# State of the delta rule by pairs of heads on the whole array, and new numbers for the planner of a hybrid decoder layer

## The chip, the core and the metric

The kernel runs on one core of one Trainium2 chip. The metric is device time in microseconds (us) of one execution. TensorE (PE) does the matmuls, ScalarE (ACT) and VectorE (DVE) do the work on elements, GpSimd (POOL) a few pieces, and SyncE (SP) issues most DMAs. "PEld" in views is PE's loading of weights.

## The reference

One decoder layer for 256 tokens and 1024 channels in float32. The input is multiplied by one large matrix; the columns feed four groups of six heads of 64 channels each: block attention (a), a state space model (s), dilated attention (c) and the gated delta rule (d). Their outputs stand side by side, are multiplied by `w_out`, added to the scaled input and normalised.

```python
proj = x @ w_in                       # (256, 1024) @ (1024, about 5,900)
y_a = moba_attention(...) * silu(a_g)
y_b = rms_norm(ssd_mixer(...) * silu(s_z), ssm_norm_w)
y_c = dilated_attention(...) * silu(c_g)
o_d = gated_delta_chunked(dq, dk, dv, d_beta, d_logdecay)
y_d = rms_norm(o_d, dn_norm_w) * silu(d_g)
mix = concatenate([y_a, y_b, y_c, y_d]) @ w_out
return layer_norm(DEEPNORM_ALPHA * x + mix, ln_g, ln_b)
```

The delta rule goes over chunks and carries a 64x64 state `St` for each head; the change is in the product that makes the state for the second chunk:

```python
v_new = uc - wc @ St
o = (qc * exp(gc)) @ St + ac @ v_new
St = St * exp(glast) + einsum("bhcd,bhce->bhde", kc * exp(glast - gc), v_new)
```

## The kernel before

**Staging.** The big products run as three: each weight block is loaded as float32 into a `raw` buffer, ACT rounds it to `whi` (fp32r), DVE subtracts to give `wlo`, and PE multiplies x high by `whi`, x low by `whi` and x high by `wlo`. There are four buffers each of `raw`, `whi` and `wlo`, so a load waits for the split of the block four before it, and a split waits until PE has read the block four before it. SP issues all these loads, and those of biases, in one fixed order. PSUM has eight banks (`ps0` to `ps7`); a tile of any kind takes a bank until its last reader is done.

**Order.** The kernel's functions do not run instructions, they record them in a `Plan`. `Plan.run` then sorts them, engine by engine, with a model of costs, and all are issued from line 381. At each step it takes an instruction by rank, which is the length of the model's work behind it plus a bias: `PRIO` gives one per stage ("attention a", "delta"), `STEPS` one per step of a stage and engine. `LIMIT` says how many banks a kind of tile may hold at once ("m" are the products of the delta rule, "g" gates, "a" scores of attention a). `AHEAD` lets an engine take a more important instruction that is ready a little later than another. `STICK` favours, on PE, an instruction that uses the same part of the array as the one before, when that is not the whole array:

```python
def stay(o):
    return int(STICK * 1000) if o["mode"] and o["mode"] == mode != (128, 128) else 0
rank = [-int(o["way"] * 1000 + 0.5) - math.floor(o["bias"] * 1000 + 0.5) for o in ops]
```

**Stages in the order of time.** "conv" and "gate" stages project the delta rule's q, k, v and its decays (to about 60 us). "products" (62 to 72 us) are twelve float32 matmuls `kq x kT` of 64 rows, each of which fills a bank that DVE turns into a block of `M` and one of `A`. Then come projections for s, c and a. "blocks" is a long chain on DVE over `Ub`, which inverts the triangular blocks (to 138 us). "attention c" (about 119 us on) and "attention a" (about 144 us on): PE makes scores, DVE adds a bias and takes the row maximum (a custom instruction that reads `biasc` or `biasa`), ACT takes the exponential and scales (`p`), PE transposes `p`. "join" (154 us on) ends the inverse: `TZ x M`, a copy of `TZ`, `U x TZ`, a copy of `U`. "delta" goes through two chunks of two halves: `vb x U` gives `u`, ACT copies it, `u x M` corrects the next half, DVE subtracts it from `vb`. After the first chunk `u x kdec` makes the state, DVE copies it to `St`, and `St x kbg` and `St x EQ` use it in the second. "out" multiplies by `w_out` (170 to 224 us), "ln" normalises and stores.

Of the kernel before, what the change touches and what calls it, by code (L numbers as in the profile page):

```python
# [16 lines left out]
S, DM, NH, HD = 256, 1024, 6, 64  # L17
W = NH * HD
# [32 lines left out]
def _biases():  # L51
# [12 lines left out]
NSM = 478  # L64
WARM = 8
STREAM = 1.0
SWITCH, PORT, AHEAD = 0.17, 0.9, {"dve": 0.033, "pe": 0.172, "pool": 0.066}
CUTS = (((0, 512), (512, 512)), ((0, 512), (512, 256), (768, 256)))
SHARE = [[slice(a, b) for a, b in v] for v in (
    ((0, 256), (256, 512)), ((512, 1024),), ((0, 512), (512, 1024)), ((0, 384), (384, 768), (768, 1024)))]  # L70
HELD = 5
HOLD = {10: (("hold_hi", "cvg", 1), ("hold_lo", "s3", 1))}
PRIO = {"split": -6.8, "conv k": 146.3, "gate d": -1265.8, "conv q": 1492.8, "gate s": 701.0, "steps": 1693.7,
        "decay d": 1542.9, "norm k": 4481.3, "products": 382.5, "norm q": 5697.9, "decay s": -3554.0,
        "values c": 663.3, "conv v": 174.6, "blocks": 42.6, "join": -2709.8, "delta": 4073.4, "conv bc": 149.8,
        "conv x": -58.8, "state": -630.8, "scan": 3483.0, "scores c": -913.9, "attention c": 9085.5,
        "scores a": 5133.5, "values a": -8452.1, "attention a": 1239.3, "out": -958.7, "out 0": -3694.0,
        "out 1": -5902.3, "ln 0": -1382.8, "ln 1": -1514.8}
CONST = -5, -4, -3
NRAW = 4  # L80
POOL = (6,)
POOLS = {"ps": (8, 512, F), "work": (3, W, F), "workd": (2, W, F), "workx": (1, W, F), "workg": (2, W, F), "cy": (3, S, F), "p": (3, W, F), "mx": (3, 4, F), "pt": (3, W, F), "oss": (2, 6, F), "sss": (2, 1, F), "srs": (2, 1, F)}
RINGS = {"raw": 4, "whi": 4, "wlo": 4}
STEPS = {"conv q 0": {"pe": -2.7}, "gate s 4": {"dve": -198.5}, "products 2": {"dve": 421.0},
# [9 lines left out]
         "attention a 5": {"dve": 0.6, "act": 142.2}, "attention a 6": {"act": -596.3},  # L94
         "attention a 10": {"act": -288.8}, "out 4": {"pe": 22.2}}
LIMIT = {"pj": 6, "g": 3, "ed": 6, "es": 6, "n": 4, "m": 5, "d": 2, "o": 4, "td": 2, "b": 1, "s": 2, "ts": 5, "c": 3, "ct": 6, "cv": 4, "a": 6, "at": 1, "av": 1}
BEGIN, SLOW = 1.2, 2.5
BESIDE = {(64, 128): 0.85, (128, 64): 0.62}
STICK = 1.0


class Plan:
# [70 lines left out]
    def add(self, eng, call, cost, outs, ins, dma=0.0, mode=None, port=False, place=None, slow=0.0):  # L173
        i = len(self.ops)
        if self.found:
            self.ops.append({"id": i, "call": call, "dma": dma})
            return
        deps = {} if self.after is None else {self.after: 0.0}
        op = {"id": i, "bias": self.bias + STEPS.get(self.step, {}).get(eng, 0.0), "stream": self.stream, "eng": eng, "call": call, "cost": cost, "dma": dma,
              "mode": mode, "port": port, "place": place, "slow": slow, "deps": deps, "succ": [], "homes": []}  # L180
# [40 lines left out]
    def run(self):  # L221
# [22 lines left out]
        vacant = {t: list(range(v[0])) for t, v in POOLS.items()}  # L244
        kinds = dict(LIMIT)
        turn = {}
# [21 lines left out]
        def stay(o):  # L268

            return int(STICK * 1000) if o["mode"] and o["mode"] == mode != (128, 128) else 0  # L270

# [120 lines left out]
def hybrid_layer(ctx, tc, plan, xT, x, w_in, w_out, convw, small, ln_g, ln_b, cst, biases, out):  # L392
    nc = tc.nc
    pe, act, dve, pool, sp = (plan.engine(n, e) for n, e in (
        ("pe", nc.tensor), ("act", nc.scalar), ("dve", nc.vector), ("pool", nc.gpsimd), ("sp", nc.sync)))
    pj = plan.engine("pe", nc.tensor, True)
# [5 lines left out]
    def part(name):  # L402
        plan.bias = PRIO.get(name, 0.0)
        plan.stage = plan.step = name

    def step(n):
        plan.step = "%s %d" % (plan.stage, n)

    def new(name, *shape, dt=F, tag=None, bufs=1):
        return plan.tile(sb, (128,) + shape, dt, name, tag, bufs)  # L410

    def bank(kind):
        return plan.tile(ps, (128, 512), F, "ps_" + kind, "ps", kind=kind)

    def work(n=W, tag="work"):
        return new(tag, W)[:, :n]

    def f32(ap):
        return ap.bitcast(F)
# [27 lines left out]
    def split(src, parts=None, tags=None):  # L447
# [3 lines left out]
                  for t, g, b in (tags or (("whi", None, 1), ("wlo", None, 1))))  # L451
        plan.bias += PRIO["split"]
        for r, c in parts or ((slice(0, k), slice(0, n)),):
            act.activation(hi[:, r, c], src[:, r, c], AF.Copy)
            (pool if count in POOL else dve).tensor_sub(lo[:, r, c], src[:, r, c], f32(hi[:, r, c]))
        plan.bias -= PRIO["split"]
        count += 1
# [33 lines left out]
    b = bank("pj")  # L491
# [244 lines left out]
    b = bank("ed")  # L736
# [6 lines left out]
    kbg, kdec = new("kbg", 3, 128), new("kdec", W)  # L743
    for i in range(2):
        b = bank("n")
# [12 lines left out]
        b = bank("n")  # L758
# [6 lines left out]
    for i in range(2):  # L765
        for pr in range(3):
            step(3 * i + pr)
            gb = [bank("m"), bank("m")]
            for g, q in zip(gb, halves):
                pe.matmul(g[:, 0:256], kT[q, pr, i * 128:(i + 1) * 128], kq[q, pr, i].rearrange("p a b -> p (a b)"),  # L770
                          start=True, stop=True)
            for e in range(2):
                h = 2 * pr + e
# [4 lines left out]
    for i in range(2):  # L778
        b, sq = bank("n"), work()
# [17 lines left out]
    for i in range(2):  # L797
        b = bank("n")
# [21 lines left out]
    for j in range(31, 0, -1):  # L820
        n = 32 - j
# [13 lines left out]
    b = bank("d")  # L835
# [5 lines left out]
    b = bank("d")  # L841
# [7 lines left out]
    u = new("u", 2, W, tag="s2")  # L849
    St = new("St", 3, 2, HD)  # L850
    pool.memset(St, 0.0)
    mix[9] = new("mix9", 2, 3, S, dt=R)
    for i in range(2):
        if i:
            b = bank("d")
            for k in range(3):
                pe.matmul(b[:, k * 128:(k + 1) * 128], kbg[:, k, :], St[:, k].rearrange("p e d -> p (e d)"),
                          start=True, stop=True)
            dve.tensor_sub(vb[:, 1, :], vb[:, 1, :], b[:, :W])
        for r in range(2):  # L860
            step(4 * i + r)
            tp = slice(64 * r, 64 * r + 64)
            if r:
                b = bank("d")
                for h in range(NH):
                    hs = slice(h * HD, h * HD + HD)
                    pe.matmul(b[tp, hs], M[0:64, 6 * i + h, tp], u[0:64, i, hs], start=True, stop=True)
                dve.tensor_sub(vb[tp, i, :], vb[tp, i, :], b[tp, :W])
            b = bank("d")
            for h in range(NH):  # L870
                hs = slice(h * HD, h * HD + HD)
                pe.matmul(b[tp, hs], U[tp, 6 * i + h, tp], vb[tp, i, hs], start=True, stop=True)
            act.activation(u[tp, i, :], b[tp, :W], AF.Copy)
        if i == 0:
            b = bank("d")
            for h in range(NH):
                q = slice(64 * (h % 2), 64 * (h % 2) + 64)
                hs = slice(h * HD, h * HD + HD)
                pe.matmul(b[q, (h // 2) * HD:(h // 2) * HD + HD], kdec[:, hs], u[:, 0, hs], start=True, stop=True)
            for e in range(2):  # L880
                q = slice(64 * e, 64 * e + 64)
                dve.tensor_copy(St[q, :, e, :], b[q, :3 * HD].rearrange("p (k d) -> p k d", k=3))
        step(4 * i + 2)
        ob = bank("o")
        for k in range(3):
            if i:
                pe.matmul(ob[:, k * 128:(k + 1) * 128], qg[:, k, :], St[:, k].rearrange("p e d -> p (e d)"),
                          start=True, stop=False, skip_group_check=True)
            for h in (2 * k, 2 * k + 1):
                hs = slice(h * HD, h * HD + HD)  # L890
                pe.matmul(ob[:, hs], A[:, 6 * i + h, :], u[:, i, hs], start=(i == 0),
                          stop=(i == 0 or h % 2 == 1), skip_group_check=True)
        sq, y = work(tag="workd"), work(tag="workd")
        ss = new("oss", 6)
        act.activation(sq, ob[:, :W], AF.Square)
        dve.tensor_reduce(ss, h6(sq), op=OP.add, axis=AX.X)
        dve.scalar_tensor_tensor(ss, ss, 1.0 / 4096, qn[:, i, :], op0=OP.mult, op1=OP.add)
        rsqrt(ss, ss)
        dve.tensor_scalar(ss, ss, 0.0625, None, op0=OP.mult)
        dve.tensor_mul(h6(y), h6(ob[:, :W]), hb(ss))  # L900
        dve.tensor_mul(y, y, gd[:, i, :])
        to_mix("d", y, i, 9)
# [13 lines left out]
    b = bank("b")  # L916
# [3 lines left out]
    b = bank("b")  # L920
# [4 lines left out]
    for i in range(2):  # L925
        for g in range(2):
            s = slice(6 * i + 3 * g, 6 * i + 3 * g + 3)
# [3 lines left out]
    for i in range(2):  # L931
        b = bank("b")
# [6 lines left out]
    b = bank("b")  # L939
    for g in range(2):  # L940
        pe.matmul(b[:, g * 192:(g + 1) * 192], btok[:, g * 128:(g + 1) * 128], Xd[:, g * 192:(g + 1) * 192],
                  start=True, stop=True)
# [3 lines left out]
    for i in range(2):  # L946
        y = yd[:, i, :]
        step(i)
        b = bank("s")
        for h in range(NH):  # L950
            hs = slice(h * HD, h * HD + HD)
            pe.matmul(b[:, hs], Es[:, 6 * i + h, :], X[:, i, hs], start=True, stop=True)
        dve.tensor_add(y, b[:, :W], y)
        if i == 1:
            b = bank("s")
            for g in range(2):
                pe.matmul(b[:, g * 192:(g + 1) * 192], bcT[:, 2 + g, 128:256], st[:, g * 192:(g + 1) * 192],
                          start=True, stop=True)
# [12 lines left out]
    bc = new("biasc", NH, 256, tag="s3")  # L971
# [131 lines left out]
```

## Time and profile before

| | |
|---|---|
| time, median of 3 runs | 232.57 us (232.31 to 232.76) |
| the profiled execution's own time | 233.04 us |
| its span, first to last instruction | 231.3 us |
| mean granted TensorE clock | 0.994 |
| busy: PE, DVE, ACT, POOL | 218.9, 174.5, 140.0, 24.2 us |
| last matmul starts at | 223.93 us |

The span is what the trace covers; 1.7 us of the execution's own time lie around it. Windows are in us from the span's start.

### The profile page before, as it was taken

The numbers are of one execution on the slowest core, as the hardware profiler recorded it, in microseconds if no ns is written. First come the engines' busy times: TensorE is split into PE (matmuls) and PEld (weight loads), VectorE is DVE, ScalarE is ACT, GpSimd is POOL, SyncE is SP. The second block draws the span as 40 slices with busy tenths as digits, with TensorE's granted clock in tenths as the row PEclk, the third lists the DMA queues.
The fourth block names the chain that finished last, engine by engine and source line by source line (L and its number), as shares of the span: only waits on it lengthen the run. The fifth ranks groups of instructions, "written<-read, shape, count | busy, mean of one in ns | idle before, by whom it ended". The sixth has DMA issues, their size and how long they took to land. (4 is left out here: it accounts for less than half of the span.)

```text
span 231.3 us, 4530 instructions
## 1 busy us (share of the span) xinstructions
PE 218.9 (95%) x1679; PEld 202.6 (88%) x1679; DVE 174.5 (75%) x414; ACT 140.0 (61%) x297; POOL 24.2 (10%) x28
## 2 busy tenths in 40 slices
PE   8999999999999999999989999798999999999970
PEld 3999899998989999999979998687889998888870
DVE  2764999998599989998999984351677996635274
ACT  4765965738953666754469936999932854442210
POOL 7005021200110000000000000000221300000071
PEclk9999999999999999999999999999999999999997
DMA  5999766893934975489550249940523052663013
GB/s 170 312 335 361 209 195 201 211 241 81 273 102 102 234 187 155 128 225 277 150 163 29 68 101 320 270 110 9 180 67 119 1 184 91 211 242 94 0 68 113
DMA packets 46101, 38.10 MB, mean 165 GB/s; under 512 B 5616, under 2 KB 42608, under 8 KB 46080
## 3 DMA queue, kind: packets, MB, share of 16 engines
q1 hardware_dynamic: 45648, 37.43, 55.2%
q10 hardware_dynamic: 432, 0.39, 0.5%
q8 instruction: 13, 0.21, 0.4%
q14 instruction: 8, 0.07, 0.1%
HBM read 36.18 MB, written 1.64 MB: 163 GB/s over the span
## 5 line engine op out<-in xcount | busy, mean ns | idle before, releaser
L381 ACT ACTIVATE whi<-raw 128x1024 fp32r<-128x1024 f32 (+3 forms) x57 | 56.9, 1004 | 40.9 <-PE ps L381 31.1
L381 DVE TENSOR_TENSOR wlo<-raw,whi 128x1024 fp32r<-128x1024 f32 (+3 forms) x56 | 64.2, 1154 | 21.3 <-ACT whi L381 17.5
L381 PE MATMUL ps<-xhi,whi 128*128 128x256 f32 x272 | 41.9, 289 | 0.2
L381 PE MATMUL ps<-xlo,whi 128*128 128x256 f32 x272 | 41.8, 286 | 0.0
L381 PE MATMUL ps<-xhi,wlo 128*128 128x256 f32 x272 | 39.8, 284 | 0.0
L381 PEld LDWEIGHTS ps<-xhi,whi 128*128 128x128 f32 x272 | 36.0, 190 | 2.6 <-ACT whi L381 1.5
L381 PEld LDWEIGHTS ps<-xlo,whi 128*128 128x128 f32 x272 | 36.4, 191 | 0.8 <-issue 0.3
L381 PEld LDWEIGHTS ps<-xhi,wlo 128*128 128x128 f32 x272 | 35.7, 189 | 0.0
L381 PE MATMUL ps<-whi,mix 128*128 128x512 f32 (+1 forms) x110 | 28.7, 350 | 0.0
L381 ACT ACTIVATE p<-p,mx 128x256 f32<-128x256 f32 (+1 forms) x48 | 19.5, 444 | 3.6 <-DVE mx L381 3.6
L381 PEld LDWEIGHTS ps<-whi,mix 128*128 128x128 f32 x110 | 19.1, 188 | 2.7
L381 DVE SCALAR_TENSOR_TENSOR cy<-ps,cw,cy 128x253 f32<-128x253 f32 (+2 forms) x48 | 20.8, 473 | 0.8 <-ACT cy L381 0.7
L381 PE MATMUL ps<-wlo,mix 128*128 128x512 f32 (+1 forms) x55 | 19.3, 350 | 0.0
L381 PE MATMUL ps<-whi,xlo 128*128 128x384 f32 (+2 forms) x64 | 17.3, 344 | 0.0
L381 PE MATMUL ps<-whi,xhi 128*128 128x384 f32 (+2 forms) x64 | 16.9, 345 | 0.0
L381 PE MATMUL ps<-wlo,xhi 128*128 128x384 f32 (+2 forms) x64 | 16.4, 340 | 0.0
L381 POOL TENSOR_SCALAR_AFFINE_SELECT Es<-Es 128x1536 f32<-128x1536 f32 x1 | 1.5, 1548 | 100.7 <-ACT Es L381 100.7
L381 PEld LDWEIGHTS ps<-whi,xlo 128*128 128x128 f32 x64 | 11.6, 188 | 0.1
L381 PEld LDWEIGHTS ps<-wlo,xhi 128*128 128x128 f32 x64 | 11.6, 188 | 0.1
L381 PEld LDWEIGHTS ps<-whi,xhi 128*128 128x128 f32 x64 | 11.2, 188 | 0.5 <-ACT whi L381 0.2
L381 PEld LDWEIGHTS ps<-wlo,mix 128*128 128x128 f32 x55 | 10.4, 188 | 1.4
L381 DVE TENSOR_TENSOR Ub<-Ub 48x31 f32<-48x31 f32 (+15 forms) x31 | 10.3, 332 | 0.7
(219 smaller groups left out, 309.4 us busy)
## 6 DMA issues: line engine op xcount, KB each, us to landing
raw<-in_w_in_dram SPq DMA_DIRECT2D x30, 512.0 KB, 4.4
raw<-in_w_out_dram SPq DMA_DIRECT2D x12, 512.0 KB, 3.4
raw<-in_w_in_dram SPq DMA_DIRECT2D x8, 384.0 KB, 3.3
lead<-in_w_in_dram SPq DMA_DIRECT2D x7, 256.0 KB, 5.0
raw<-in_w_in_dram SPq DMA_DIRECT2D x4, 396.0 KB, 6.6
raw<-in_w_in_dram SPq DMA_DIRECT2D x4, 390.0 KB, 4.7
x<-in_x_dram SPq DMA_DIRECT2D x2, 512.0 KB, 5.1
xr<-in_xT_dram SPq DMA_DIRECT2D x7, 128.0 KB, 5.0
```

Source lines behind the costliest of these rows:

```text
L381: self.plan.add(eng, lambda: f(*a, **k), cost, outs, ins, dma, mode, port or (eng == "pool" and not dma), place, slow)
```

## The change

The state's product takes two heads at a time: three matmuls of the whole 128x128 array in place of six of a 64 column part. The blocks off the diagonal, products of one head's keys with the other's values, are made and not read: the two copies to `St` take the diagonal. A step mark is gone. All tables of the planner have new values; a few lines of them stand here.

```diff
-SWITCH, PORT, AHEAD = 0.17, 0.9, {"dve": 0.033, "pe": 0.172, "pool": 0.066}
+SWITCH, PORT, AHEAD = 0.17, 0.9, {"pe": 0.175}
...
-LIMIT = {"pj": 6, "g": 3, "ed": 6, "es": 6, "n": 4, "m": 5, "d": 2, "o": 4, "td": 2, "b": 1, "s": 2, "ts": 5, "c": 3, "ct": 6, "cv": 4, "a": 6, "at": 1, "av": 1}
+LIMIT = {"pj": 5, "g": 6, "ed": 5, "es": 5, "n": 3, "m": 4, "d": 4, "o": 5, "td": 2, "b": 1, "s": 1, "ts": 4, "c": 6, "ct": 3, "cv": 4, "a": 5, "at": 1, "av": 1}
...
-STICK = 1.0
+STICK = 1000.0
...
         if i == 0:
             b = bank("d")
-            for h in range(NH):
-                q = slice(64 * (h % 2), 64 * (h % 2) + 64)
-                hs = slice(h * HD, h * HD + HD)
-                pe.matmul(b[q, (h // 2) * HD:(h // 2) * HD + HD], kdec[:, hs], u[:, 0, hs], start=True, stop=True)
+
+            for k in range(3):
+                c = slice(k * 128, k * 128 + 128)
+                pe.matmul(b[:, c], kdec[:, c], u[:, 0, c], start=True, stop=True)
             for e in range(2):
                 q = slice(64 * e, 64 * e + 64)
-                dve.tensor_copy(St[q, :, e, :], b[q, :3 * HD].rearrange("p (k d) -> p k d", k=3))
-        step(4 * i + 2)
+                dve.tensor_copy(St[q, :, e, :], b[q, :W].rearrange("p (k a d) -> p k a d", k=3, a=2)[:, :, e, :])
```

The order moves in most stages between 27 us and 201 us; the first 159 and the last 123 instructions of PE stand as before. Three places are shown. Numbers behind names are those of buffers.

On PE the products stood in three groups, five, six and one, between projections. Before:

```order
L381 MATMUL ps3_97<-kq_94,kT_93 128x256
L381 MATMUL ps7_120<-kq_94,kT_93 128x256
L381 MATMUL ps2_99<-kq_94,kT_93 128x256
L381 MATMUL ps5_105<-kq_94,kT_93 128x256
L381 MATMUL ps6_106<-kq_94,kT_93 128x256
L381 MATMUL ps1_96<-xhi_87,whi_187 128x256
L381 MATMUL ps0_86<-xhi_87,whi_190 128x256 x8
L381 MATMUL ps0_86<-xlo_88,whi_190 128x256 x8
L381 MATMUL ps0_86<-xhi_87,wlo_191 128x256 x8
L381 MATMUL ps6_106<-kq_94,kT_93 128x256
L381 MATMUL ps4_98<-kq_94,kT_93 128x256
```

After, the same place:

```order
L381 MATMUL ps6_106<-kq_94,kT_93 128x256
L381 MATMUL ps2_99<-kq_94,kT_93 128x256
L381 MATMUL ps3_97<-kq_94,kT_93 128x256
L381 MATMUL ps5_105<-kq_94,kT_93 128x256
L381 MATMUL ps0_86<-xhi_87,whi_187 128x256 x8
L381 MATMUL ps0_86<-xlo_88,whi_187 128x256 x8
L381 MATMUL ps0_86<-xhi_87,wlo_188 128x256 x2
L381 MATMUL ps1_96<-kq_94,kT_93 128x256
L381 MATMUL ps7_120<-kq_94,kT_93 128x256
L381 MATMUL ps4_98<-kq_94,kT_93 128x256
L381 MATMUL ps6_106<-kq_94,kT_93 128x256
```

Four products now stand ahead of 18 matmuls of a projection, and eight in a row follow (four more behind those shown).

On DVE, ahead of attention a, the splits `wlo_298` and `wlo_301` stood apart in the chain over `Ub`. SP issues the load `raw_308` when the first is done, `raw_311` when the second is, and then `biasa`, the biases that attention a adds. Before:

```order
L381 TENSOR_TENSOR wlo_298<-raw_296,whi_297 128x768
L381 TENSOR_TENSOR work1_155<-ps6_106,cg_164 128x256
L381 TENSOR_TENSOR Ub_202<-BL_201,Ub_202 48x156
L381 TENSOR_TENSOR Ub_202<-Ub_202 48x6x26
L381 TENSOR_TENSOR Ub_202<-BL_201,Ub_202 48x135
L381 TENSOR_TENSOR work2_156<-ps4_98,cg_164 128x256
L381 TENSOR_TENSOR Ub_202<-Ub_202 48x5x27
L381 TENSOR_TENSOR Ub_202<-BL_201,Ub_202 48x112
L381 TENSOR_TENSOR Ub_202<-Ub_202 48x4x28
L381 TENSOR_TENSOR Ub_202<-BL_201,Ub_202 48x87
L381 TENSOR_TENSOR wlo_301<-raw_299,whi_300 128x768
```

After, the same place:

```order
L381 TENSOR_TENSOR Ub_202<-BL_201,Ub_202 48x156
L381 TENSOR_TENSOR work1_155<-ps2_99,cg_164 128x256
L381 TENSOR_TENSOR Ub_202<-Ub_202 48x6x26
L381 TENSOR_TENSOR Ub_202<-BL_201,Ub_202 48x135
L381 TENSOR_TENSOR Ub_202<-Ub_202 48x5x27
L381 TENSOR_TENSOR Ub_202<-BL_201,Ub_202 48x112
L381 TENSOR_TENSOR work2_156<-ps7_120,cg_164 128x256
L381 TENSOR_TENSOR Ub_202<-Ub_202 48x4x28
L381 TENSOR_TENSOR wlo_301<-raw_299,whi_300 128x768
L381 TENSOR_TENSOR Ub_202<-BL_201,Ub_202 48x87
L381 TENSOR_TENSOR wlo_298<-raw_296,whi_297 128x768
```

Both splits now stand late in the chain, `wlo_301` first, and SP issues `raw_311`, `raw_308` and `biasa` in that order.

On PE, join and delta, from the copy of `U` to the state's use. Before:

```order
L381 MATMUL ps3_97<-xhi_87,whi_309 128x256
L381 MATMUL ps5_105<-vb_195,U_196 64x64 x6
L381 MATMUL ps3_97<-xhi_87,whi_309 128x256 x5
L381 MATMUL ps6_106<-u_204,M_157 64x64 x6
L381 MATMUL ps3_97<-xhi_87,whi_309 128x256 x2
L381 MATMUL ps3_97<-xlo_88,whi_309 128x256 x4
L381 MATMUL ps5_105<-vb_195,U_196 64x64 x6
L381 MATMUL ps4_98<-xhi_87,whi_312 128x256 x6
L381 MATMUL ps6_106<-u_204,kdec_153 64x64 x6
L381 MATMUL ps5_105<-u_204,A_158 128x64 x4
L381 MATMUL ps2_99<-St_205,kbg_152 128x128 x3
```

After, the same place:

```order
L381 MATMUL ps7_120<-xhi_87,whi_309 128x256 x6
L381 MATMUL ps3_97<-vb_195,U_196 64x64 x6
L381 MATMUL ps7_120<-xhi_87,whi_309 128x256 x2
L381 MATMUL ps7_120<-xlo_88,whi_309 128x256 x3
L381 MATMUL ps4_98<-u_204,M_157 64x64 x6
L381 MATMUL ps7_120<-xlo_88,whi_309 128x256 x5
L381 MATMUL ps7_120<-xhi_87,wlo_310 128x256
L381 MATMUL ps3_97<-vb_195,U_196 64x64 x6
L381 MATMUL ps7_120<-xhi_87,wlo_310 128x256 x7
L381 MATMUL ps6_106<-xhi_87,whi_312 128x256 x5
L381 MATMUL ps4_98<-u_204,kdec_153 128x128 x3
L381 MATMUL ps3_97<-u_204,A_158 128x64 x5
```

The matmuls `St x kbg` follow the five of `A`. Ahead of `vb x U`, `u x M` and the state there are now 6, 5 and 18 matmuls of projections in place of 1, 5 and 12. On ACT the split `whi_322`, of a block of `w_out` that is wanted later, now stands ahead of the second copy of `u`; on DVE its `wlo_323` stands ahead of the copies to `St`.

## Rows read from the trace of the kernel before

**Rows 1.** The page, busy time and share of the span of each engine.
```profile
PE 218.9 (95%) x1679; PEld 202.6 (88%) x1679; DVE 174.5 (75%) x414; ACT 140.0 (61%) x297; POOL 24.2 (10%) x28
```
**Rows 2.** What PE waited for: total us, times, longest.
```profile
PE ps L381 <- ACT p L381: 2.7, 3, 1.2
```
**Rows 3.** Timeline of PE at conv q: start, busy us, instruction, [idle before].
```profile
26.85 0.51 PE L381 MATMUL ps<-xlo,whi 128*128 128x256 f32 x3
27.47 1.22 PE L381 MATMUL ps<-xhi,whi 128*128 128x256 f32 x8
```
**Rows 4.** Timeline of DVE and PE around the decays' transposes.
```profile
53.63 1.23 DVE L381 TENSOR_TENSOR wlo<-raw,whi 128x1024 fp32r<-128x1024 f32 x1 [0.70 <-ACT whi L381]
...
54.85 0.16 DVE L381 COPY cumd<-ps 128x12 f32<-128x12 f32 x1
...
55.16 0.38 PE L381 MATMUL ps<-csb,cumd 128*6 128x128 f32 x2 [0.47 <-DVE cumd L381]
```
**Rows 5.** Timeline of PE at the products; each product shows as two rows.
```profile
61.81 1.11 PE L381 MATMUL ps<-xhi,wlo 128*128 128x256 f32 x8
62.85 1.56 PE L381 MATMUL ps<-kq,kT 64*128 64x256 f32 x10
...
67.49 1.73 PE L381 MATMUL ps<-kq,kT 64*128 64x256 f32 x12
69.15 1.09 PE L381 MATMUL ps<-xhi,whi 128*128 128x256 f32 x7
70.18 0.70 PE L381 MATMUL ps<-kq,kT 64*128 64x256 f32 x2
70.80 1.22 PE L381 MATMUL ps<-xlo,whi 128*128 128x256 f32 x8
```
**Rows 6.** Timeline of DVE at the products.
```profile
64.10 1.46 DVE L381 TENSOR_TENSOR wlo<-raw,whi 128x1024 fp32r<-128x1024 f32 x1 [0.52 <-ACT whi L381]
...
66.32 1.11 DVE L381 SCALAR_TENSOR_TENSOR M<-ps,rk,Ed 128x128 f32<-128x128 f32 x4
```
**Rows 7.** Timelines of DVE, SP, ACT and PE ahead of attention a.
```profile
132.75 0.96 DVE L381 TENSOR_TENSOR wlo<-raw,whi 128x768 fp32r<-128x768 f32 x1
...
138.24 0.34 SPq L381 DMA_DIRECT2D biasa<-in_biases_dram  x1
...
144.05 0.42 DVE L381 CUSTOM_DVE_ANT_0 p<-ps,biasa 128x256 f32<-128x256 f32 x1 [0.83 <-DMA biasa<-in_biases_dram]
...
144.52 0.51 ACT L381 ACTIVATE p<-p,mx 128x256 f32<-128x256 f32 x1 [2.02 <-DVE mx L381]
...
147.13 0.55 PE L381 MATMUL ps<-csb,p 128*128 128x128 f32 x3 [1.24 <-ACT p L381]
```
**Rows 8.** DMA issues from 130 to 150 us: count, KB each, us from issue to landing.
```profile
raw<-in_w_in_dram SPq DMA_DIRECT2D x3, 512.0 KB, 4.3
biasa<-in_biases_dram SPq DMA_DIRECT2D x1, 768.0 KB, 5.7
```
**Rows 9.** Timeline of PE in join and delta.
```profile
160.16 0.91 PE L381 MATMUL ps<-vb,U 64*64 64x64 f32 x12 [0.54 <-ACT U L381]
...
162.12 0.91 PE L381 MATMUL ps<-u,M 64*64 64x64 f32 x12 [0.27 <-ACT u L381]
...
165.71 0.57 PE L381 MATMUL ps<-u,kdec 128*64 128x64 f32 x12
166.21 1.10 PE L381 MATMUL ps<-u,A 128*128 128x64 f32 x8
167.37 0.94 PE L381 MATMUL ps<-St,kbg 128*128 128x128 f32 x6
168.14 0.56 PE L381 MATMUL ps<-u,A 128*128 128x64 f32 x4
```
**Rows 10.** Timelines of ACT and DVE in delta.
```profile
165.68 1.06 ACT L381 ACTIVATE whi<-raw 128x1024 fp32r<-128x1024 f32 x1
...
166.32 0.72 DVE L381 COPY St<-ps 64x192 f32<-64x192 f32 x2 [1.29 <-PE ps L381]
```

More of the change, by code (lines that the diff above doesn't have):

```diff
@@ L72 @@
 HOLD = {10: (("hold_hi", "cvg", 1), ("hold_lo", "s3", 1))}
[L73 to L78, printed above, removed]
+PRIO = {"split": -6.8, "conv k": -839.0, "gate d": -1623.0, "conv q": 3038.6, "gate s": 708.5, "steps": 2655.8,
+        "decay d": 1955.6, "norm k": 4396.4, "products": 252.7, "norm q": 5719.5, "decay s": -3877.9,
+        "values c": 581.4, "conv v": 156.6, "blocks": -701.0, "join": -3665.0, "delta": 5543.6, "conv bc": 87.4,
+        "conv x": -23.6, "state": -57.6, "scan": 4309.6, "scores c": -1661.9, "attention c": 8479.5,
+        "scores a": 4875.0, "values a": -8056.3, "attention a": 113.3, "out": -847.7, "out 0": -3284.5,
+        "out 1": -7153.9, "ln 0": -1284.1, "ln 1": -492.7}
 CONST = -5, -4, -3
@@ L83 @@
 RINGS = {"raw": 4, "whi": 4, "wlo": 4}
-STEPS = {"conv q 0": {"pe": -2.7}, "gate s 4": {"dve": -198.5}, "products 2": {"dve": 421.0},
[9 rows of a table removed]
-         "attention a 5": {"dve": 0.6, "act": 142.2}, "attention a 6": {"act": -596.3},
-         "attention a 10": {"act": -288.8}, "out 4": {"pe": 22.2}}
-LIMIT = {"pj": 6, "g": 3, "ed": 6, "es": 6, "n": 4, "m": 5, "d": 2, "o": 4, "td": 2, "b": 1, "s": 2, "ts": 5, "c": 3, "ct": 6, "cv": 4, "a": 6, "at": 1, "av": 1}
+STEPS = {"gate s 3": {"dve": 111.0}, "gate s 4": {"dve": -194.3}, "products 2": {"dve": 332.3},
[11 rows of a table added]
+LIMIT = {"pj": 5, "g": 6, "ed": 5, "es": 5, "n": 3, "m": 4, "d": 4, "o": 5, "td": 2, "b": 1, "s": 1, "ts": 4, "c": 6, "ct": 3, "cv": 4, "a": 5, "at": 1, "av": 1}
 BEGIN, SLOW = 1.2, 2.5
 BESIDE = {(64, 128): 0.85, (128, 64): 0.62}
-STICK = 1.0
+STICK = 1000.0
 class Plan:
```

20 rows, old and new, of the table STEPS are left out of this document.

## The prediction

> **What bounds the kernel now.** I read the page first. TensorE is busy for 95% of the span [rows 1], so time is won only where PE stands still, where it changes the part of the array that it uses, or where it has less to do. The view of waits comes next: its largest item is 2.7 us in three stops for ACT's exponentials [rows 2]. The timeline of PE then places the stops: 1.24 us at attention a's first transpose [rows 7], 0.54 and 0.27 in join and delta [rows 9], 0.47 at the decays' transposes [rows 4], and a start at 27.47 that is late against the pace [rows 3]. That pace: eight matmuls of 256 columns take from 61.81 to 62.85 [rows 5], less about 0.1 for the switch at the end, so 0.118 us each; by columns one of 384 takes 0.177.
>
> The stops have late partners, and these decide what a new order is worth. At attention a DVE waits for the transfer of `biasa` and starts at 144.05; ACT starts at 144.52 [rows 7], and its timeline shows no idle row from there to the second copy of `u`, which ends at about 165.7, where the next split starts [rows 10]. The state's product starts on PE at 165.71 [rows 9]. So from 144 to 166 us ACT's queue is the chain, and PE's stops are where it catches up with that queue. A stop that is filled with other matmuls comes back at the next copy, unless ACT's work ahead of that copy is shorter too.
>
> **The state's product.** Twelve rows take from 165.71 to 166.21, 0.50 us [rows 9]. After the change there are three matmuls of 128 columns on the whole array, six rows; the nearest row is `St x kbg`, the same shape, six rows from 167.37 to 168.14, 0.77 us (with a restart of about 0.1 taken off it is 0.67). Bounds: 0.67 to 0.77, so a loss of 0.17 to 0.27. The change of array part in front of it goes; what that is worth is bounded by zero and by a whole excursion, 0.41 (below). I take half, 0.2, and get a loss of about 0.05. The copies to `St` keep their size, two in 0.72 [rows 10]; what is read is strided otherwise, for which no row has a price: I take nothing, with 0.1 as an upper bound.
>
> The Trainium skill (TensorEngine Tiling (Array Packing), Performance Considerations) offers 2x for a tiled output of 64 columns, which speaks against this change: by that rule the whole-array form would take 1.0 us, and the sum below would be 0.25 lower, a forecast of 232.8. By the rows it is 0.77 at most: the tiled form gains a factor of 1.3 to 1.5 here and not 2, and the sum stays as it is below.
>
> **Conv q.** After three matmuls from 26.85 the next was due at 27.20 and starts at 27.47 [rows 3], 0.27 late, for a split on ACT. After the change the first block's 24 matmuls run on. That gains 0 to 0.37 (with a restart of 0.1). The splits on ACT keep their order and PE arrives at the next one sooner, so I take 0.15.
>
> **Decays.** PE waits 0.47 for `cumd`, which stands on DVE behind a split of 1.23 us begun at 53.63 [rows 4]. In the order after, this split is still ahead, and five matmuls of 384 in place of six lie between. That costs 0.18; one split of the stage is also moved later on DVE, and with it the load behind it. Range -0.6 to 0, taken -0.25.
>
> **Products.** Two rows take 0.62 (70.18 to 70.80), twelve take 1.66 (67.49 to 69.15) [rows 5]: 0.104 a row and 0.41 for going there and back. Two excursions in place of three save 0.41. Against this, each product needs two DVE operations, four of which take 1.11 [rows 6], so about 0.53 a product where PE needs 0.21. DVE begins after the split that starts at 64.10 and takes 1.46, at 65.5. The last of the eight needs bank `ps1` again, which the first of the eight used: eight operations of the first four products and three more come before it is free, at 65.5 + 11 x 0.265 = 68.4. PE comes there at 62.85 + 0.2 + 8 x 0.104 + 0.2 + 18 x 0.118 + 0.2 + 14 x 0.104 = 67.9. So it waits about 0.5 (0 to 0.8). Net -0.1.
>
> **Attention a.** PE has ten matmuls of 384 in place of five between the last work of the scores and the first transposed `p`. That covers 0.88 of the 1.24 and is worth nothing by itself, since the chain is ACT's. What counts is when `biasa` lands. It is issued at 138.24 [rows 7] and takes 5.7 us [rows 8]. Before, the load `raw_308` could go out at about 133.7, after a split begun at 132.75 and lasting 0.96 [rows 7], and with 4.3 us [rows 8] it landed at about 138.0, before `biasa` was issued. Now it goes out only after `wlo_298`, late in the chain over `Ub`, right before `biasa`: 512 KB more in front of it. But `raw_311`, of the same size, goes out earlier. If the two merely trade places the cost is 0; if not, 256 KB more cost 5.7 - 4.3 = 1.4 us by rows 8, so 512 KB up to 2.8. The exchange is the nearer case; I take -0.15.
>
> **Join and delta.** Until the second copy of `u` ACT does what it did before and one split more, 1.06 [rows 10]: the state can start 1.0 later. By then PE has done 29 matmuls of 256 columns where it had done 18 (11 x 0.118 = 1.30), so the work stands 0.3 further on. The stops for `U` and `u`, 0.54 and 0.27, are covered or paid on the way there and aren't counted again. Behind the state, `St x kbg` began 0.22 late (eight rows of `A` from 166.21 at 0.117 end at 167.15; start 167.37) [rows 9]; five matmuls of `A` in place of four, 0.23, cover that: +0.2. On DVE `wlo_323` now stands before the copies to `St`; its split is the one ahead of `u` on ACT, and it ends near 167.4, when the product is done too. Taken together +0.5, from -0.4 (the split late by a DVE slot) to +1.1.
>
> **Out.** PE shows no stop there; four splits stand in another order, and POOL's order is unchanged. Taken -0.05 (-0.3 to 0.2).
>
> **The sum.** -0.05 + 0.15 - 0.25 - 0.1 - 0.15 + 0.5 - 0.05 = 0.05 us gained: nothing that counts. The profiled execution takes 233.04, 0.47 more than the median of the runs, 232.57; the same difference applies to both kernels, so I forecast **232.5 us**.
>
> **Rivals.**
> *The stops all add up.* If ACT's chain starts earlier or has slack that I don't see, the covered 0.88 of attention a, the 0.54 and 0.27 of join and delta with 0.1 of restart each, 0.3 of conv q, 0.4 of an excursion and 0.2 at `kbg` give 2.8 us: 229.8; half of it, 231.2. For it speaks that each of these has more cover in the new order; against it, ACT's rows without idle time from 144.52 on. Chance 0.36 for any gain above 0.2%, of which 0.2 for more than 1 us.
> *`biasa` lands late.* One mechanism: `raw_308` is in front of `biasa` in SP's queue and not over when it starts. It shifts DVE's first row at 144.05, ACT's chain and the state's start one for one. With half of 2.8, 1.4: 233.9. It decides from the point where DVE's first bias operation starts 0.5 later than 144.05 relative to the last `Ub` operation. Chance 0.15.
> The Trainium skill (DMA: Bandwidth & Descriptors, Queues, rings and completion order) says that descriptors on each DMA engine are consumed in ring order, all of SP's from one row of rings. That speaks for this rival; no row here shows two loads in that order yet.
> *Waits at products and decays are larger.* Taking the lower ends, -0.8 + 0.41 and -0.6, in place of -0.35: 0.65 lost, 233.1. Chance 0.1.
> *The state does nothing.* Its bounds, -0.27 to +0.24, are near what can be told apart, so this is inside the forecast and not a case apart: the time comes from the order.
>
> **Chances.** A change of 0.2%, 0.47 us, is about the least that a measurement of this kernel can tell from none. No change: 0.39. Faster: 0.37, slower: 0.24, from the rivals and the tails of the terms. The range 231.1 to 233.6 holds half of the first rival's gain and most of the second's price. The forecast's own range is 232.1 to 233.0.
>
> **What would show it.** The state as six rows in about 0.7 us with no array change before it; two excursions at the products, the second with a stop of about 0.5 before its last product; at conv q no start off the pace at 27 us; at attention a a first stop of 0.3 to 0.7 in place of 1.24, and ACT again without idle time until `u`; a stop of 0.5 or so at `vb x U` or `u x M`; the state's start 0.7 to 1.2 later by the clock, with more matmuls behind it. The forecast is wrong if ACT's chain begins or ends more than 0.5 from where I have it, or if a stop appears among the projections of s, c and a or in out, where PE now has none.

## The result and the profile after

The changed kernel takes 234.25 us (median of 12 runs, 233.13 to 235.85) beside 232.75 us for the kernel before in the same runs. The ratio is 1.0095, with an interval of 1.0069 to 1.0121: about 2.2 us slower, where no change was forecast and 233.6 was the upper end. The profiled execution has a span of 232.3 us. Slow runs are left out of every ratio (here three of the kernel before, 235.74 us and more; the median of its other nine is 232.57), and the profiles of two runs below have stretches at a granted clock of 0.5 (1.2 GHz), so that of one (`b_split_late`) only what lies ahead of 148 us is read and of the other (`b_behind`) no stretch.

The page and the list of waits after, which answer to [rows 1, 2]:

```profile
PE 219.4 (94%) x1673; PEld 202.6 (87%) x1673; DVE 175.4 (75%) x414; ACT 140.0 (60%) x297; POOL 23.6 (10%) x28
...
PE ps L381 <- ACT p L381: 2.3, 3, 1.1
PE ps L381 <- DVE mx L381: 1.2, 1, 1.2
```

Every engine is about as busy as before. The waits for `p` are shorter, and one of 1.2 us is new: a projection's matmul waits for DVE. The timelines of SP, DVE, ACT and PE ahead of attention a show why; they answer to [rows 7]:

```profile
138.23 0.35 SPq L381 DMA_DIRECT2D biasa<-in_biases_dram  x1
...
145.08 0.42 DVE L381 CUSTOM_DVE_ANT_0 p<-ps,biasa 128x256 f32<-128x256 f32 x1 [2.01 <-DMA biasa<-in_biases_dram]
...
145.55 0.51 ACT L381 ACTIVATE p<-p,mx 128x256 f32<-128x256 f32 x1 [3.17 <-DVE mx L381]
...
144.16 0.38 PE L381 MATMUL ps<-csb,cums 128*6 128x128 f32 x2
145.78 0.61 PE L381 MATMUL ps<-whi,xhi 128*128 128x384 f32 x2 [1.23 <-DVE mx L381]
...
148.65 0.55 PE L381 MATMUL ps<-csb,p 128*128 128x128 f32 x3 [0.87 <-ACT p L381]
```

`biasa` is issued at the same time as before (138.23; before 138.24), 0.01 ahead of the last operation on `Ub` in both, but DVE's first operation on it comes at 145.08 and not at 144.05, with 2.01 us of waiting for that one transfer. ACT's chain starts 1.03 later. PE's new stop has the same origin: the ten matmuls that were to cover the first `p` need a bank of scores that DVE hasn't read yet (with one load moved, `a_one_behind` below, they start at 143.70 without a stop). The end is 1.01 later as well (last matmul 224.94, before 223.93). The view of DMAs from 130 to 150 us, first after, then before (busy share of the 16 DMA engines in slices of 0.5 us, then issue to landing):

```profile
DMA  0058930010000058999699999999999998987899
...
raw<-in_w_in_dram SPq DMA_DIRECT2D x3, 512.0 KB, 5.6
biasa<-in_biases_dram SPq DMA_DIRECT2D x1, 768.0 KB, 6.7
```
```profile
DMA  0047940004699600169999989998999999889999
```

Before, one load runs from about 134.5 to 137 us and is out of the way. After, nothing moves from 133 to 137, and then two loads of 512 KB and `biasa` go one behind the other; `biasa` lands 6.7 us after its issue in place of 5.7 [rows 8].

### The profile page after: what moved, and what is told of

The parts are those of the page before. It is cut to its first block, busy times and chain, and to the rows that moved or that the text cites. A ratio compares the mean times of both kernels' runs of the same rounds, so it can differ in the third digit from the quotient of the medians.

```text
span 232.3 us, 4514 instructions
## 1 busy us (share of the span) xinstructions
PE 219.4 (94%) x1673; PEld 202.6 (87%) x1673; DVE 175.4 (75%) x414; ACT 140.0 (60%) x297; POOL 23.6 (10%) x28
## 4 chain that ended last, share of the span: by engine, by line
PE 69%; ACT 14%; DVE 7%; DMA 6%; issue 2%; DVEq 0%; ACTq 0%
PE ps L381 69%; ACT p L381 4%; ACT whi L381 4%; DMA biasa<-in_biases_dram 3%; DVE wlo L381 2%; DMA raw<-in_w_in_dram 2%; ACT Es L381 2%; ACT Ed L381 2%; DMA xr<-in_xT_dram 1%; DVE r L381 1%; DVE p L381 1%; DVE M L381 1%; DVE A L381 1%; ACT pt L381 1%; DVE Ub L381 0%
## 5 line engine op out<-in xcount | busy, mean ns | idle before, releaser
L381 DVE TENSOR_TENSOR wlo<-raw,whi 128x1024 fp32r<-128x1024 f32 (+3 forms) x56 | 65.3, 1174 | 19.4 <-ACT whi L381 18.2
L381 ACT ACTIVATE whi<-raw 128x1024 fp32r<-128x1024 f32 (+3 forms) x57 | 56.8, 1004 | 33.1 <-PE ps L381 23.2
L381 PE MATMUL ps<-xhi,whi 128*128 128x256 f32 x272 | 43.7, 288 | 0.7 <-ACT Es L381 0.4
L381 PE MATMUL ps<-xlo,whi 128*128 128x256 f32 x272 | 43.0, 286 | 0.0
L381 PE MATMUL ps<-xhi,wlo 128*128 128x256 f32 x272 | 42.3, 284 | 0.0
L381 PEld LDWEIGHTS ps<-xhi,whi 128*128 128x128 f32 x272 | 37.1, 190 | 2.6 <-ACT whi L381 1.5
L381 PEld LDWEIGHTS ps<-xlo,whi 128*128 128x128 f32 x272 | 37.4, 191 | 0.3 <-DVE xlo L381 0.2
L381 PEld LDWEIGHTS ps<-xhi,wlo 128*128 128x128 f32 x272 | 36.8, 190 | 0.4 <-issue 0.3
L381 ACT ACTIVATE cy<-ps,cw 128x256 f32<-128x256 f32 x16 | 8.7, 553 | 7.6 <-PE ps L381 3.3
```

Source lines behind the costliest of these rows:

```text
L381: self.plan.add(eng, lambda: f(*a, **k), cost, outs, ins, dma, mode, port or (eng == "pool" and not dma), place, slow)
```

## The experiments

Theory 1: the loss is that landing. Both loads now wait for splits that stand late on DVE, and 1 MB goes right ahead of `biasa`. Theory 2: the loss lies in the new order on PE and ACT from attention a on (the banks of scores, the split ahead of the second copy of `u`).

A name that begins with `a_` is a run of the changed kernel with an edit, one with `b_` a run of the kernel before with an edit. The table has three stretches of each profile, from the starts of rows of the timelines, so that the start of an execution doesn't blur them: from attention c's first score matmul (`cqk`) to DVE's first bias operation; from the first bias operation to the state's product; and, again from the first bias operation, to the last matmul. Up to the state's product the new order does 1.30 us more of projections than the old one.

| run | ratio (interval) | `cqk` to first bias | first bias to state | first bias to last matmul |
|---|---|---|---|---|
| before | 1 | 26.21 | 21.65 | 79.87 |
| after | 1.0095 (1.0069 to 1.0121) | 27.34 | 22.73 | 79.86 |
| after_again | 1.0091 (1.0055 to 1.0128) | 27.40 | 22.73 | 79.81 |
| a_one_behind | 1.0015 (0.9989 to 1.0040) | 25.81 | 22.74 | 79.81 |
| a_both_behind | 1.0013 (0.9993 to 1.0033) | 25.68 | 22.74 | 79.86 |
| b_late | 1.0007 (0.9982 to 1.0031) | 26.06 | 21.67 | 79.91 |
| b_split_late | 1.0090 (1.0052 to 1.0128) | 27.44 | | |
| b_state | 1.0044 (1.0014 to 1.0074) | 26.77 | 21.67 | 80.05 |
| b_behind | 0.9968 (0.9940 to 0.9996) | | | |
| b_behind_again | 0.9965 (0.9929 to 1.0002) | 25.47 | 21.69 | 79.93 |
| b_state_behind | 0.9976 (0.9944 to 1.0007) | 25.59 | 21.65 | 80.04 |
| a_oldstate_behind | 1.0000 (0.9970 to 1.0031) | 25.58 | 22.75 | 79.83 |
| a_products2 | 1.0041 (1.0010 to 1.0071) | 25.76 | 22.76 | 79.85 |

The last column is the first reading: from DVE's first bias operation to the last matmul it is 79.8 to 80.05 us in every kernel. Where only the loads move, in one order of PE, the end follows the first bias operation one for one. That the two orders of PE agree as well (79.87 and 79.86) is a balance of a gain and a loss (below).

**The loads moved behind `biasa`, in the changed kernel.** Added to the planner, after its order is made; `n` is 1 in the first run and 2 in the second:

```diff
+        sp = [i for i in order if ops[i]["eng"] == "sp"]
+        b = ...  # place of the load of biasa
+        for i in sp[b - n:b]:
+            order.remove(i)
+        order[order.index(sp[b + 1]) + 1:order.index(sp[b + 1]) + 1] = sp[b - n:b]
```

> The changed kernel; only SP's order differs: the load raw_308 goes out behind biasa and dU, not right before biasa, so that one load of 512 KB (raw_311) is left ahead of biasa, as before the change. Theory 1 (the loss is biasa landing late, because both loads now go out right before it): DVE's first bias operation comes back from 145.1 to about 144.0 us, ACT's chain and the end follow one for one, the kernel is 1.0 us or more faster than the changed one and the ratio to the kernel before falls from 1.0095 to about 1.000 to 1.005. Theory 2 (the loss is in the new order on PE, ACT and DVE: values' matmuls that wait for banks of scores, one more split ahead of the second copy of u): biasa lands earlier, but the ratio stays at 1.008 or more.

> The changed kernel with raw_311 and raw_308 both behind biasa and dU on SP, nothing ahead of biasa. Theory 1: biasa lands another 1 us or more earlier, the first bias operation at about 142.5 to 143.3 (then bound by PE's scores), the chain of ACT up to 2 us earlier than in the changed kernel; ratio 0.993 to 0.999, faster than the kernel before. Theory 2: 1.005 or more.

DVE's first bias operation in the two runs:

```profile
142.98 0.42 DVE L386 CUSTOM_DVE_ANT_0 p<-ps,biasa 128x256 f32<-128x256 f32 x1 [0.52 <-PE ps L386]
```
```profile
143.45 0.42 DVE L386 CUSTOM_DVE_ANT_0 p<-ps,biasa 128x256 f32<-128x256 f32 x1 [0.33 <-DMA biasa<-in_biases_dram]
```

With one load behind, DVE no longer waits for the transfer but for PE's scores. Either run takes 1.5 to 1.7 us off the stretch up to the first bias operation and 0.8% off the time. Theory 1 holds for that part: nothing on PE, ACT or DVE was touched. Theory 2 finds nothing from the first bias operation on, where the stretch is as long as before; what remains ahead of it is taken up under the sum below. The second load brings nothing more, and neither kernel beats the one before, against what was expected of the second.

**The two loads exchanged on SP, in the kernel before.**

```diff
+        order.remove(sp[b - 2])
+        order.insert(order.index(sp[b - 1]) + 1, sp[b - 2])
```

> The kernel before; only SP's order differs: raw_308 goes out behind raw_311, right before biasa, as in the changed kernel. Theory 1: first bias operation from 144.05 to about 145.1, 1.0 us slower, ratio 1.004 to 1.010. Theory 2: no difference, 1.000.

No difference, but the edit didn't bring about what it was for. The two issues stand 4.50 and 0.86 us ahead of `biasa`'s (133.01, 136.65, 137.51) as they did before: by these times a load took whichever buffer was freed first, so only the blocks changed places, not the times. It speaks neither for nor against.

**One split moved on DVE, in the kernel before.**

```diff
+        u = ...  # DVE's split wlo_298
+        w = ...  # DVE's split wlo_301
+        order.remove(u)
+        order.insert(order.index(w) + 1, u)
```

> The kernel before; on DVE the split wlo_298 stands right behind wlo_301, as late as in the changed kernel, and nothing else is moved. So the first of the two 512 KB loads can go out only at about 136 us, not at 133.7, and both stand right before biasa (what the run with the two loads exchanged on SP did not bring about: a load takes whichever buffer is freed first, and the first went out as early as before). Theory 1 (biasa lands late because 1 MB is right ahead of it): first bias operation 1.0 to 1.8 later after biasa's issue than the 5.3 to 6.2 us seen with the kernel before, ratio 1.004 to 1.010. Theory 2 (the loss lies in the order on PE and ACT from attention a on): 0.999 to 1.002.

SP and DVE in this run:

```profile
136.72 1.24 SPq L386 DMA_DIRECT2D raw<-in_w_in_dram  x2
138.46 0.59 SPq L386 DMA_DIRECT2D biasa<-in_biases_dram  x1
...
144.62 0.42 DVE L386 CUSTOM_DVE_ANT_0 p<-ps,biasa 128x256 f32<-128x256 f32 x1 [1.82 <-DMA biasa<-in_biases_dram]
```

One DVE instruction, placed ten places later in the otherwise old order, costs what the whole change costs: 1.0090. But the cost came another way than expected. From issue to first use it is 6.16 us, within the 5.25 to 6.25 of the old order, where 1.0 to 1.8 more was expected. What is later is the issue: it stands at the last operation on `Ub`, and that is 0.9 later than before, counted from `cqk` or from the load ahead of the three. DVE shows why; the split had filled two waits for PE, which now stand open:

```profile
132.47 0.42 DVE L386 TENSOR_TENSOR work<-ps,cg 128x256 f32<-128x256 f32 x1 [0.38 <-PE ps L386]
...
134.31 0.42 DVE L386 TENSOR_TENSOR work<-ps,cg 128x256 f32<-128x256 f32 x1 [0.53 <-PE ps L386]
```

So this run shows again that the arrival of `biasa` sets the end, but not that two loads ahead of it make its transfer longer; in the changed kernel the issue isn't late.

**The changed kernel once more.**

> The changed kernel itself once more, beside the other three, to see how far its time and the landing of biasa vary from one execution to another. Both theories: ratio 1.005 to 1.012; first bias operation 6.0 to 6.9 us after biasa's issue.

It gives the same ratio, and the first bias operation 6.9 us after the issue (145.23, issue 138.31).

**The kernel before with nothing right ahead of `biasa`,** by the first edit with `n` = 1, twice:

> The kernel before with raw_311 behind biasa and dU on SP, so that no load is right ahead of biasa. Theory 1: first bias operation about 5.2 after biasa's issue, near the moment at which PE has the first scores; ACT's chain starts 0.3 to 1.0 earlier and the end follows: ratio 0.995 to 0.999. Theory 2: 1.000.

> The kernel before with raw_311 behind biasa once more, beside the others: whether the gain of 0.3% holds. Theory 1: ratio 0.994 to 0.999, first bias operation 5.0 to 5.3 after biasa's issue.

DVE's first bias operation in the second of them:

```profile
142.64 0.42 DVE L386 CUSTOM_DVE_ANT_0 p<-ps,biasa 128x256 f32<-128x256 f32 x1
```

No row shows a wait: the stretch up to it is 0.6 to 1.3 less than the three profiles in the old order of DMAs (25.47; 26.06 to 26.77), 0.3% faster. It is the only order tried that beats both kernels; its second interval just reaches 1.

**The state by pairs of heads alone,** each other instruction at its old place, without and with the load behind `biasa`:

```diff
-                pe.matmul(b[q, (h // 2) * HD:(h // 2) * HD + HD], kdec[:, hs], u[:, 0, hs], start=True, stop=True)
+                pe.matmul(b[:, c], kdec[:, c], u[:, 0, c], start=True, stop=True)   # three in place of six
```

> The kernel before in its own order on every engine, only the state's product by pairs of heads (three matmuls of the whole array, copies from the diagonal). Theory 1: 0.67 to 0.77 us in place of 0.50 for the product, the change of array part in front of it gone; time within 0.3 us of before, ratio 0.999 to 1.001. Rival (the state itself costs: St comes later and everything behind it waits): 1 us slower, 1.004 or more.

> As the one before it, with the state's product by pairs of heads as well. The difference of the two is the price of the state's product where biasa's landing does not blur it. By the trace of the run with the state alone (state's start to St x kbg 1.84 us in place of 1.66): 0.1 to 0.3 us slower than its neighbour, 0.0005 to 0.0015 in the ratio. If the state costs what the run with the state alone showed in its times: 0.004.

The timeline of PE with the state alone answers to [rows 9]:

```profile
165.45 0.94 PE L381 MATMUL ps<-u,kdec 128*128 128x128 f32 x6
166.22 1.00 PE L381 MATMUL ps<-u,A 128*128 128x64 f32 x8
167.29 0.91 PE L381 MATMUL ps<-St,kbg 128*128 128x128 f32 x6
```

The product takes 0.77 in place of 0.50, and the wait for `St` behind it is 0.09 shorter than in the run with the loads exchanged; from the state to `St x kbg` it is 1.84 in place of 1.66. From the second `vb x U` to the state it is 1.85 with either form, so no change of array part was saved in front. In the table the last stretch is 0.11 to 0.18 longer. That is the state's price, and between the runs with the load moved the ratio differs by 0.001. The 1.0044 without it is more than that; in its profile `biasa` landed late (26.77), 0.4 above the mean of the old order, which may be some of the rest, as far as one profile can tell.

**The old state in the changed kernel,** both loads behind `biasa`:

```diff
-                pe.matmul(b[:, c], kdec[:, c], u[:, 0, c], start=True, stop=True)
+                two(k, b)   # the two matmuls of this pair of heads, as before
...                              # the copies to St read as before, too
```

> The changed kernel with both loads behind biasa and the old state (six matmuls of a part of the array), order otherwise unchanged. By the pair of runs on the kernel before, the pairs of heads cost 0.18 us between the state's start and St x kbg; here this stretch gets 0.1 to 0.2 shorter than the 2.07 of the run with both loads behind, or stays, if what St x kbg waits for is the split ahead of the copies to St. Ratio 1.000 to 1.002.

From the state to `St x kbg` it is 2.08 us with either form, and the end is the same. In the new order the state's form costs nothing, because `St x kbg` waits for something else (below).

**The products in three groups of four,** in the changed kernel with both loads behind `biasa`, first with the matmuls alone moved:

```diff
+        late = kq[8:12]
+        at = order.index(pq[n + 14]) + 1
+        order[at:at] = late
```

> The changed kernel with both loads behind biasa, and the last four of the eight products in a row moved behind the next 14 matmuls of projections: three groups of four in place of four and eight. If the products' own price is DVE falling behind (the eight took 3.19 us in the changed kernel, where 0.41 and 16 rows at 0.104 make 2.07), the wait of 1.1 us goes and an array change of 0.41 comes back: from the decays' transposes to attention c's first scores 0.6 to 0.7 shorter (62.4 in place of 63.05 us), ratio 0.996 to 1.000. If DVE's lateness moves on to the next banks: still 62.9 or more and the ratio as without it, 1.001.

In this first form DVE stands ahead of the moved matmuls and makes `M` and `A` of the last four products from what the banks held before; PE then waits for DVE (1.11 us) and the ratio of 1.0074 (1.0038 to 1.0110) tells nothing of the question. In the second form DVE's operations on them are moved too:

```diff
+        for i in part:
+            if late & set(ops[i]["deps"]):
+                late.add(i)
```

> As the run with the products in three groups of four, with DVE's operations on the four moved products behind them in the program too. If the products' own price is DVE falling behind: from the decays' transposes to attention c's first scores 62.4 us in place of 63.05, ratio 0.996 to 1.000. If DVE's lateness moves on to the next banks: 62.9 or more, ratio 1.001.

The timeline of PE in the second form, then of DVE:

```profile
69.22 1.21 PE L395 MATMUL ps<-xhi,whi 128*128 128x256 f32 x8 [0.21 <-DVE A L395]
70.37 1.13 PE L395 MATMUL ps<-kq,kT 64*128 64x256 f32 x8
...
71.10 1.13 DVE L395 SCALAR_TENSOR_TENSOR M<-ps,rk,Ed 128x128 f32<-128x128 f32 x4 [0.90 <-PE ps L395]
```

From the decays' transposes to attention c it takes 63.80 us, longer than the 63.05 without the move. The long stop before the last product is gone, but DVE now waits 0.90 for PE and ends its 24 operations 1.0 later. Behind that DVE's rows show no gap up to 80 us, and PE stops once for it (0.30 at 98.30). The second alternative's number holds, and more than was expected of it, but its mechanism only in part: PE stops 0.21 for DVE at 69.22, while the larger wait is that of DVE for PE.

## Why the prediction was wrong

**The step that failed** is the term for attention a, "The exchange is the nearer case; I take -0.15". It measured -1.0 (27.37 against a mean of 26.35 in the three profiles with the old order on DVE and SP). I had seen that `raw_308` would go out right before `biasa`, and set against it that `raw_311` would go out earlier. But that one came 1.27 us earlier (136.11 in place of 137.38) while the other came 3.63 later (137.37 in place of 133.74), and the queue stood empty in between. The two didn't trade places: 512 KB that had been moved by 137 were now in front of `biasa`. The rival "`biasa` lands late", to which I gave 0.15, is what happened: DVE's first bias operation came 1.04 us later behind the last operation on `Ub`, past the 0.5 from which it was to decide. Its price of 1.4 was nearer than my own term. The Trainium skill (DMA: Bandwidth & Descriptors, Queues, rings and completion order) has each DMA engine consume descriptors in ring order; the runs agree in direction: from issue to first use it is 6.9 us in the changed kernel with both loads right ahead and 6.2 in `b_split_late`, 5.25 to 6.25 with one, and 4.9 to 5.2 with none. One load and two aren't told apart by every profile; the runs that moved loads alone tell the cause.

**What bounds the stretch** was read rightly: ACT's chain from the first bias operation on, not PE's stops. After the change ACT's timeline again has no idle row, from 145.55 to 170.1 us. Up to the state's product the new order takes 1.08 us longer (22.73, before 21.65), as one more split of 1.06 on ACT was to make it, though PE has more work to fill its stops with. The rival that all stops add up got nothing.

**The other terms.** In the trace after, as [rows 3 to 5, 9, 10] before:

```profile
26.40 1.11 PE L381 MATMUL ps<-xlo,whi 128*128 128x256 f32 x8
27.35 1.11 PE L381 MATMUL ps<-xhi,wlo 128*128 128x256 f32 x8
...
54.70 0.38 PE L381 MATMUL ps<-csb,cumd 128*6 128x128 f32 x2 [0.17 <-DVE cumd L381]
...
62.45 1.14 PE L381 MATMUL ps<-kq,kT 64*128 64x256 f32 x8
...
65.84 3.26 PE L381 MATMUL ps<-kq,kT 64*128 64x256 f32 x16
69.03 0.98 PE L381 MATMUL ps<-xhi,wlo 128*128 128x256 f32 x6
...
167.81 0.94 PE L381 MATMUL ps<-u,kdec 128*128 128x128 f32 x6
168.59 1.23 PE L381 MATMUL ps<-u,A 128*128 128x64 f32 x10
...
169.89 0.91 PE L381 MATMUL ps<-St,kbg 128*128 128x128 f32 x6
```

Conv q has no late start, as forecast. The decays' stop is 0.17 here, but 0.10 to 0.59 over the profiles of the new order and 0.10 to 0.52 over those of the old one; what conv q gave and the decays took can't be told from the start's own variation (last section). From the decays' transposes to attention c, where both kernels do the same work, the changed one takes 63.05 us and the old one 62.69 (three profiles within 0.02): 0.36 lost, of which 0.26 from the first product to the last, projections between them taken off at 0.118 (0.1 forecast). The eight products took 3.19 us where 2.07 would do without a wait, a wait of 1.1 and not of 0.5. My sum also left out that the old order lost 0.5 to waits in its three groups; that the net came near (0.1 forecast, 0.26 measured) is the luck of two errors that offset each other. Splitting the eight didn't win the wait back, as the last run shows.

Join and delta: the state starts 1.08 later behind the first bias operation with 1.30 more done, 0.22 gained where 0.3 was forecast. The 0.2 behind it, and the 0.05 for the state, came out as a loss of 0.18: state to `St x kbg` took 2.08 in place of 1.66, of which the fifth matmul of `A` is 0.23. Together that is 0.04 where 0.45 was forecast, the second term that was mis-sized. DVE shows what was late:

```profile
167.28 1.71 DVE L381 TENSOR_TENSOR wlo<-raw,whi 128x1024 fp32r<-128x1024 f32 x1 [0.93 <-ACT whi L381]
169.02 0.72 DVE L381 COPY St<-ps 64x192 f32<-64x192 f32 x2
```

The split that I let end near 167.4 in my own terms began at 167.28, since the whole chain was late, and took 1.71 in place of 1.23 beside an operation of POOL (last section); the copies to `St` stand behind it. For the state's product the Trainium skill (TensorEngine Tiling (Array Packing), Theoretical Speedup) gives a dimension of 64 a speedup of up to 2x, by which I estimated twice the tiled form's 0.50; it is 0.77, the upper of my two bounds.

**The sum.** In the profiles 0.36 is lost up to attention c, 1.0 up to the first bias operation and nothing behind: 1.4 us. The runs say 2.1, with intervals that begin at 1.3 and 1.6. The rest is 0.7 by the middle and 0.2 by the nearer end. The runs with nothing right ahead of `biasa` say where it isn't: even so the new order stands behind the old one, 1.0013 beside 0.9976 with pairs of heads, 1.0000 beside 0.9965 and 0.9968 with the old state. That is 0.8 to 0.9 us by the middles (the intervals touch), of which the profiles show the 0.36 ahead of attention c and little else. So the landing is a little over half of the loss, the new order ahead of attention a is some of what is left, and the remainder stays open; there is one profile to each kernel's twelve or so runs.

## What to carry to other kernels

A transfer that a whole stage waits for belongs ahead of bulk loads that have time, and its price is read from when the bytes ahead of it move, not from how many loads stand in the queue. Moving one instruction on an engine that frees buffers moves the loads behind them; follow each of these to the queue and to what shares it. Stops of a busy engine that another engine's chain causes aren't won by filling them: look for the stretch whose length stays when its start is moved.

## What the runs showed of the hardware that I had not expected

The same program starts differently from one execution to the next: PE's 141st matmul starts between 23.2 and 25.0 us in the 14 profiles, and all these kernels have the same order on PE up to there. The landing of `biasa` behind the same loads varies by 1 us (first use 5.25 to 6.25 after the issue in before, b_late and b_state). And DVE's splits of 128x1024 take longer beside an affine select of POOL. Of the 574 in the 14 profiles, the 553 with none beside them take 1.20 to 1.23 us. The 14 that share 0.38 us with one take 1.45 or 1.46 (the split at 64.10 in [rows 6] is one of them), and the 7 that share 0.63 us take 1.70 or 1.71; these are the splits ahead of the copies to `St`, one in each profile of the new order. No run moved the POOL operation to test it, but no such split is long without it. In the trace after it is this one:

```profile
166.36 1.55 POOL L381 TENSOR_SCALAR_AFFINE_SELECT Es<-Es 128x1536 f32<-128x1536 f32 x1 [102.27 <-ACT Es L381]
```
